# Transformer block on one core: ten steps of the second modulation placed ahead of the first projection group, and the last output tile summed in two column halves

## Chip, cores and metric

One core of one Trainium2 chip. The metric is the device time of one execution in microseconds (us); lower is better. Before the change three timed executions gave 676.25, 676.32 and 678.70 us, median 676.32 us.

## What is computed

One transformer block in fp32 for 512 tokens of width 1024. `D_FF` is 2816. The heads are of three kinds (six with a forget gate, four mLSTM, six block-sparse); only the frame matters here:

```python
mod = jax.nn.silu(c) @ w_ada[l] + b_ada[l]
sh1, sc1, g1, sh2, sc2, g2 = jnp.split(mod[:, None, :], 6, axis=-1)
hn = (_rms(x, norm1_g[l]) * (1 + sc1) + sh1).astype(x.dtype)
y = _mixer(hn, w_in[l], ...)
x = x + g1 * (y.astype(x.dtype) @ w_out[l])
hn = (_rms(x, norm2_g[l]) * (1 + sc2) + sh2).astype(x.dtype)
gate, up = jnp.split(hn @ w_gate_up[l], 2, axis=-1)
x = x + g2 * ((jax.nn.silu(gate) * up) @ w_down[l])
```

The six parts of `mod` are six products of one 1024-vector with 1024x1024 blocks of `w_ada`.

## The kernel before

**Stages.** (1) To about 56 us: the loads of `x`, the first norm, `sh1` and `sc1` on TensorE (PE) from tiles `ada`, and the products for the mLSTM q and k (tile `gT`). Inside this stage each engine's instructions are chained in program order. (2) To about 310 us: 70 numbered steps. Group `A` (mLSTM v and gates) is steps 0 to 7, `F0` to `F2` steps 8 to 31, `B0` to `B2` 32 to 55, `E` 56 to 63, `o0` 64 to 69. A step loads one 128-row weight tile some steps ahead (three are loaded before step 0, `PRE`), splits it into a high part on ScalarE (ACT) and a low part on VectorE (DVE) or GpSimd (POOL), and issues a share of its group's matmuls. Every product is three matmuls (high by high, high by low, low by high: `mm3`). Between the matmuls, `attend` releases the attention and mLSTM work by a table of due times, and `extra` the convolution (`cy`), the gate chain and others. (3) The second norm and the feed-forward, and (4) the down projection, which multiplies by `g2` and adds `x`.

**The second modulation.** The generator `ada` makes `g1` (`ada_row`), then `sc2` and `sh2` (`ada_col`). Each comes in two halves of 512 columns. A half is eight products: a load of 128x512 (256 KB) by SyncE (SP) into one of three buffers (`AST = 3`, tag `ast`), and a DVE instruction that multiplies it by a column of `cs` and, from the second on, adds it to the sum (the first is a TENSOR_SCALAR, the other seven are SCALAR_TENSOR_TENSOR). The ninth step of a half of `g1` loads and adds its bias row; in `sc2` and `sh2` it is empty. The next step starts with one matmul (or four small ones) over the finished sum and its copy out, then the first product of the next half. In all there are 54 steps; in the trace the halves are `g10s`, `g11s`, `sc20s`, `sc21s`, `sh20s`, `sh21s` (loads), and `g`, `sc`, `sh` (sums). From step `ADA0 = 12` on each step of the main loop takes one of them, so the last is taken at step 65.

**Order.** Outside stage 1 the engine queues are filled by the Tile framework's list scheduler, which works on its own estimate of time: of what it holds to be ready on an engine, the instruction that comes first in the program goes first. The place in the program is therefore a rank and not a time, and an instruction can run well ahead of its step. On the chip each queue then runs in the order fixed at build time, waits included. DMAs for stage 2 are all issued by SP.

**The last tile.** `down(j, t)` issues the `mm3` of inner tile `j` (22 of them) for token tile `t` (4) into PSUM bank `gg[t]`. The last `DLAST = 4` inner tiles are done token tile by token tile, so that one tile's output can leave while the next is computed. For the last tile of the second column half, the output (multiply by `g1b`, which by then holds `g2`; add `x1`; store) is in two halves of 256 columns, both after all its matmuls.

Of the kernel before, what the change touches and what calls it, by code (L numbers as in the profile page):

```python
# [18 lines left out]
NT = SEQ // P  # L19
# [3 lines left out]
NJ = DFF // P  # L23
# [16 lines left out]
POSTD = 3.0  # L40
LAG = 3.0
ADA0 = 12
OKT = (0, 1, 2, 5, 3, 4)
PTB = 2
ELEAD = 0.8
# [13 lines left out]
DLAST = 4  # L59
# [71 lines left out]
def hybrid_block_kernel(  # L131
# [6 lines left out]
    V, S, G, TE, SY = nc.vector, nc.scalar, nc.gpsimd, nc.tensor, nc.sync  # L138
    dbg = dbg or {}
    in_order = {k: [1] for k in "VSGTY"}  # L140
    V, S, G, TE, SY = (_InOrder(tc, e, in_order[k]) for e, k in zip((V, S, G, TE, SY), "VSGTY"))
# [62 lines left out]
        for f in rsqrt_ops(y, v, tag):  # L204
            f()

    def mm3(o, ah, al, wh, wl, start, stop):
        TE.matmul(o, ah, wh, start=start, stop=False)
        TE.matmul(o, ah, wl, start=False, stop=False)
        TE.matmul(o, al, wh, start=False, stop=stop)  # L210

    g1b = cp.tile([P, D], F32, name="g1b")
    mod2 = cp.tile([P, 2, 8], F32, name="mod2")
# [342 lines left out]
    def gates_4(Mr):  # L556

        pM = bank("t", "pM")
        for t in range(NT):
            TE.transpose(pM[:, t * 4:(t + 1) * 4], Mr[:, t * P:(t + 1) * P], ident[0:4, 0:4])  # L560
        V.tensor_tensor(em, Fc[:, :, 0:4], pM[:, 0:16].rearrange("p (t g) -> p t g", t=NT), op=ALU.add)
        S.activation(em, em, AF.Exp, scale=-1.0)
        gs["em"] = em
# [39 lines left out]
    def ada_all():  # L603
        yield from ada_row(2 * D, g1b, "g1")
        yield from ada_col(4 * D, "sc2", 0)
        yield from ada_col(3 * D, "sh2", 1)

    ada = ada_all()
# [293 lines left out]
    def add_x1(t, hf_, pb, eng):  # L902
        hs = slice(512 * hf_, 512 * hf_ + 512)
        tm = hp.tile([P, 512], F32, tag="P1", name=f"ot{t}{hf_}", bufs=SB)
        V.tensor_tensor(tm, pb, g1b[:, hs], op=ALU.mult)
        eng.tensor_tensor(x1[t][hf_], x1[t][hf_], tm, op=ALU.add)

    def wo(kc, hf_):
        return w_out[0, kc * P:(kc + 1) * P, 512 * hf_:512 * hf_ + 512]
# [13 lines left out]
    for pr in range(3):  # L923
        add_qkv("B", BQ, pr)
    add_group("E", KTS, lambda kt: w_in[0, kt * P:(kt + 1) * P, MO:MO + 256], 256, hn, after_e)
    add_group("o0", OKT, lambda kt: wo(kt, 0), 512, lambda kt: yT[kt],
              lambda t, pb: add_x1(t, 0, pb, G if O0G else V), BLKO0)
# [16 lines left out]
    for i in range(3):  # L944
        plan_softmax("B", i, 40 + 8 * i, gq8[:, 1:2], prmT[:, 87:88], lambda h: (AL, h), 5 + i)
    queue.sort(key=lambda e: e[:2])
    extra = {GT[0]: [g12], GT[1]: [g3], GT[2]: [g4], GT[3]: [lambda: gates_4(gs["M"])],
             len(steps) - len(OKT) + 2: [load_x1]}
    for m, j in zip((0, 2, 1, 3), CVS):
# [12 lines left out]
    def load_67(hf_):  # L962
        rr = hp.tile([P, 2, 512], F32R, tag="raw", name=f"olr{hf_}", bufs=2)
        load_late(6, hf_, (rr[:, 0], rr[:, 1]))
        load_late(7, hf_, (pairt(f"olh{hf_}"), pairt(f"oll{hf_}")))

    loads = [l for l, _ in steps]
    loads += [lambda: load_67(0)] + [lambda kt=kt: load_late(kt, 1) for kt in OKT] + [lambda: load_67(1)]
    for j in range(PRE):
        loads.pop(0)()  # L970
    for j, (_, half) in enumerate(steps):
        for _ in range(1 if j < len(steps) - LPR else 2):
            loads and loads.pop(0)()
        attend(j)
        half(0)
        attend(j + 0.5)
        for f in extra.get(j, []):
            f()
        half(1)
        if j >= ADA0:  # L980
            next(ada, None)
# [13 lines left out]
    def last_o(t):  # L995
        tsl = slice(t * P, (t + 1) * P)
        for hf_, kts, tag in ((0, (6, 7), "t"), (1, OKT + (6, 7), "g")):
            pb = bank(tag, f"ol{t}{hf_}")
# [103 lines left out]
    def temp(name):  # L1102
        return act_tile(name, F32)
# [216 lines left out]
    for hf_ in range(2):  # L1320
        gg = [bank(tg, f"d{hf_}{t}") for t, tg in enumerate(("gggg", "sstt")[hf_])]

        def down(j, t, hf_=hf_, gg=gg):
            if j % 2 == 0:
                k = NJ // 2 * hf_ + j // 2
                down_load(k + DLD)
                down_split(k + DPR)
            if steps_[0] % 2:
                next(ada2, None)
            steps_[0] += 1  # L1330
            tsl = slice(t * P, (t + 1) * P)
            ah, al, wh, wl = dprep[hf_, j]
            mm3(gg[t], ah[:, tsl], al[:, tsl], wh, wl, j == 0, j == NJ - 1)

        for j in range(NJ - DLAST):
            for t in range(NT):
                down(j, t)
        for t in range(NT):
            for j in range(NJ - DLAST, NJ):
                down(j, t)  # L1340
            parts = 2 if hf_ and t == NT - 1 else 1
            for c_ in range(parts):
                n = 512 // parts
                o = slice(c_ * n, c_ * n + n)
                ho = slice(512 * hf_ + c_ * n, 512 * hf_ + c_ * n + n)
                ot = temp(f"fo{hf_}{t}{c_}")
                V.tensor_tensor(ot[:, :n], gg[t][:, o], g1b[:, ho], op=ALU.mult)
                V.tensor_tensor(ot[:, :n], ot[:, :n], x1[t][hf_][:, o], op=ALU.add)
                SY.dma_start(out[0, t * P:(t + 1) * P, ho], ot[:, :n])
# [39 lines left out]
```

## Time and profile before

| | us |
|---|---|
| median of three runs | 676.32 |
| the profiled execution, own time | 678.59 |
| its span in the trace | 676.8 |
| PE busy | 646.9 (96%) |
| DVE busy | 518.1 (77%) |
| ACT busy | 365.1 (54%) |
| POOL busy | 97.2 (14%) |

The span is what the trace shows of the profiled execution; 1.79 us of its time lie outside of it. A time in a row is counted from the span's start. "Idle before" names what ended the wait ahead of an instruction. PE records overlap, because a matmul starts before the one ahead has drained: the distance from start to start is what one costs in a stream.

### The profile page before, as it was taken

The numbers are of one execution on the slowest core, as the hardware profiler recorded it, in microseconds if no ns is written. First come the engines' busy times: TensorE is split into PE (matmuls) and PEld (weight loads), VectorE is DVE, ScalarE is ACT, GpSimd is POOL, SyncE is SP. The second block draws the span as 40 slices with busy tenths as digits, with TensorE's granted clock in tenths as the row PEclk, the third lists the DMA queues.
The fourth block names the chain that finished last, engine by engine and source line by source line (L and its number), as shares of the span: only waits on it lengthen the run. The fifth ranks groups of instructions, "written<-read, shape, count | busy, mean of one in ns | idle before, by whom it ended". The sixth has DMA issues, their size and how long they took to land.

```text
span 676.8 us, 11779 instructions
## 1 busy us (share of the span) xinstructions
PE 646.9 (96%) x4238; PEld 588.9 (87%) x4238; DVE 518.1 (77%) x1034; ACT 365.1 (54%) x722; POOL 97.2 (14%) x135
## 2 busy tenths in 40 slices
PE   4999899999999999999999999999999999999997
PEld 3678888899999988778999999999999998788885
DVE  3549889969998899888778987888777999448313
ACT  4445478656876777645834554554544665316210
POOL 3012216344252355000000000000000000000000
PEclk9999988999999999999999999999999999999999
DMA  9986736667877667621346433322433237306101
GB/s 270 306 244 166 189 94 145 169 176 205 199 219 180 177 197 189 222 87 33 109 156 219 125 125 125 113 60 78 125 125 126 100 120 225 148 15 214 51 0 62
DMA packets 95549, 99.64 MB, mean 147 GB/s; under 512 B 8186, under 2 KB 70010, under 8 KB 95492
## 3 DMA queue, kind: packets, MB, share of 16 engines
q1 hardware_dynamic: 95492, 98.91, 50.3%
q8 instruction: 33, 0.54, 0.4%
q14 instruction: 24, 0.20, 0.1%
HBM read 84.15 MB, written 2.10 MB: 127 GB/s over the span
## 4 chain that ended last, share of the span: by engine, by line
PE 64%; DVE 19%; ACT 5%; DMA 5%; issue 4%; SPq 2%; POOL 0%; DVEq 0%; ACTq 0%; POOLq 0%
PE d L114 14%; PE B L114 5%; PE F L114 4%; PE ol L114 3%; PE gT L114 2%; DVE g L114 2%; SPq L114 2%; PE f9A L114 1%; PE f8A L114 1%; PE f7A L114 1%; PE f6A L114 1%; PE f5A L114 1%; PE f4A L114 1%; PE f3A L114 1%; PE pc L114 1%
## 5 line engine op out<-in xcount | busy, mean ns | idle before, releaser
L114 ACT ACTIVATE ah<-A 128x512 fp32r<-128x512 f32 x44 | 25.6, 620 | 33.4 <-PE d L114 33.1
L114 DVE TENSOR_TENSOR al<-A,ah 128x512 fp32r<-128x512 f32 x44 | 29.1, 685 | 18.1 <-ACT ah L114 18.1
L114 DVE TENSOR_TENSOR r<-r,r 128x1024 f32<-128x1024 f32 x20 | 24.4, 1220 | 1.5 <-DMA r<-in_w_gate_up_dram 1.2
L114 DVE TENSOR_TENSOR fo<-d,g1b 128x512 f32<-128x512 f32 (+1 forms) x9 | 5.6, 630 | 17.9 <-PE d L114 17.8
L114 ACT ACTIVATE Fp<-Fs,Fmn 128x128 f32<-128x128 f32 (+3 forms) x24 | 12.6, 526 | 9.8 <-DVE Fmn L114 5.6
L114 ACT ACTIVATE u<-u 128x512 f32<-128x512 f32 x20 | 12.5, 627 | 8.1 <-DVE u L114 8.0
L114 ACT ACTIVATE Bp<-Bs,Bmn 128x128 f32<-128x128 f32 (+3 forms) x24 | 12.6, 526 | 7.4 <-DVE Bmn L114 3.5
L114 DVE SCALAR_TENSOR_TENSOR m<-pc,b1sc,prmT 128x1 f32<-128x1 f32 x8 | 1.7, 218 | 19.1 <-PE pc L114 15.7
L114 POOL TENSOR_SCALAR Fp<-Fp,Fls 128x128 f32<-128x128 f32 (+2 forms) x18 | 11.1, 618 | 26.4 <-DVE Fls L114 21.3
L114 PE MATMUL gT<-sq,ident 128*128 128x256 f32 x12 | 5.3, 626 | 9.1 <-ACT sq L114 9.1
L114 DVE TENSOR_TENSOR A<-u,u 128x512 f32<-128x512 f32 x20 | 13.7, 684 | 0.0
L114 POOL TENSOR_SCALAR Bp<-Bp,Bls 128x128 f32<-128x128 f32 (+2 forms) x16 | 8.2, 510 | 34.4 <-DVE Bls L114 25.0
L114 DVE CUSTOM_DVE_ANT_0 Bs<-Bs,mask 128x128 f32<-128x128 f32 (+3 forms) x24 | 11.6, 492 | 1.6 <-PE Bs L114 1.6
L114 DVE TENSOR_TENSOR Bptl<-Bpt,Bpth 128x128 fp32r<-128x128 f32 (+3 forms) x24 | 11.5, 483 | 1.7 <-ACT Bpth L114 1.5
L114 ACT ACTIVATE Fpth<-Fpt 128x128 fp32r<-128x128 f32 (+3 forms) x24 | 10.4, 435 | 4.2 <-PE Fpt L114 4.1
L114 PEld LDWEIGHTS gT<-sq,ident 128*128 128x128 f32 x12 | 3.8, 329 | 10.0 <-issue 9.1
L114 DVE CUSTOM_DVE_ANT_0 Fs<-Fs,mask 128x128 f32<-128x128 f32 (+3 forms) x24 | 11.7, 488 | 1.0 <-PE Fs L114 1.0
L114 POOL TENSOR_TENSOR sml<-E,smh 128x512 fp32r<-128x512 f32 (+1 forms) x8 | 9.0, 1126 | 23.6 <-ACT smh L114 23.6
L114 PE MATMUL Bpt<-ident,Bp 128*128 128x128 f32 x60 | 10.8, 277 | 1.3 <-POOL gmo L114 0.5
L114 ACT ACTIVATE Bpth<-Bpt 128x128 fp32r<-128x128 f32 (+3 forms) x24 | 10.3, 433 | 3.2 <-PE Bpt L114 2.9
L114 DVE TENSOR_TENSOR Fptl<-Fpt,Fpth 128x128 fp32r<-128x128 f32 (+3 forms) x24 | 11.6, 484 | 0.5 <-ACT Fpth L114 0.4
L114 ACT ACTIVATE row<-pc 128x256 f32<-128x256 f32 x8 | 3.1, 382 | 15.7 <-PE pc L114 15.7
(2326 smaller groups left out, 2830.0 us busy)
## 6 DMA issues: line engine op xcount, KB each, us to landing
r<-in_w_gate_up_dram SPq DMA_DIRECT2D x40, 512.0 KB, 3.8
dr<-in_w_down_dram SPq DMA_DIRECT2D x22, 512.0 KB, 5.5
ada<-in_w_ada_dram SPq DMA_DIRECT2D x16, 512.0 KB, 7.2
x<-in_x_dram SPq DMA_DIRECT2D x4, 512.0 KB, 5.6
w0s<-in_w_in_dram SPq DMA_DIRECT2D x8, 256.0 KB, 6.6
g10s<-in_w_ada_dram SPq DMA_DIRECT2D x8, 256.0 KB, 3.6
g11s<-in_w_ada_dram SPq DMA_DIRECT2D x8, 256.0 KB, 2.7
sc20s<-in_w_ada_dram SPq DMA_DIRECT2D x8, 256.0 KB, 4.0
```

The source lines that it names most:

```text
L114: r = f(*a, **k)
```

## The change

Ten calls of `next(ada)` stand between the three early weight loads and the main loop: the eight products of the first half of `g1`, its bias, and then its matmul and copy together with the first product of the second half. The main loop is not changed, so that from step 12 on each step takes what ten steps later took before, and the last is taken at step 55. In the down projection, `down` takes a column range; the last four inner tiles are issued inside the loop over the column parts. For all tiles but the last that is the same order. For the last tile the twelve matmuls of 512 columns become twelve of 256 columns, the output of that half, twelve of 256 columns, the output of the other half. `skip_group_check` is an argument for the builder and no instruction.

```diff
+ADAE = 10
@@
-    def mm3(o, ah, al, wh, wl, start, stop):
-        TE.matmul(o, ah, wh, start=start, stop=False)
+    def mm3(o, ah, al, wh, wl, start, stop, **kw):
+        TE.matmul(o, ah, wh, start=start, stop=False, **kw)
...
     for j in range(PRE):
         loads.pop(0)()
+    for _ in range(ADAE):
+        next(ada)
     for j, (_, half) in enumerate(steps):
@@
-        def down(j, t, hf_=hf_, gg=gg):
+        def down(j, t, o=slice(0, 512), hf_=hf_, gg=gg):
@@
-            mm3(gg[t], ah[:, tsl], al[:, tsl], wh, wl, j == 0, j == NJ - 1)
+            mm3(gg[t][:, o], ah[:, tsl], al[:, tsl], wh[:, o], wl[:, o], j == 0, j == NJ - 1,
+                skip_group_check=hf_ * NT + t == 2 * NT - 1)
@@
         for t in range(NT):
-            for j in range(NJ - DLAST, NJ):
-                down(j, t)
             parts = 2 if hf_ and t == NT - 1 else 1
             for c_ in range(parts):
                 n = 512 // parts
                 o = slice(c_ * n, c_ * n + n)
+                for j in range(NJ - DLAST, NJ):
+                    down(j, t, o)
```

## Rows read from the trace of the kernel before

**Rows 1.** Stretches: stretch, then busy us (instructions) per engine, PE clock, DMA share, GB/s.

```profile
57.00:67.00 10.00, 10.00 (x82) 10.00 (x81) 9.75 (x18) 6.43 (x14) 1.85 (x2) 1.00 0.73 194
67.00:82.00 15.00, 13.97 (x90) 13.35 (x89) 11.29 (x40) 7.03 (x19) 2.95 (x3) 1.00 0.83 215
82.00:92.00 10.00, 8.62 (x41) 8.02 (x40) 8.90 (x15) 5.87 (x17) 3.98 (x3) 0.83 0.46 131
245.00:260.00 15.00, 13.40 (x100) 11.80 (x99) 14.90 (x35) 12.15 (x30) 10.40 (x14) 1.00 0.84 227
270.00:285.00 15.00, 13.69 (x72) 10.53 (x71) 12.52 (x36) 10.13 (x24) 0.85 (x2) 1.00 0.69 233
```

**Rows 2.** Chain that ended last, 240 to 280 us: start, us, work.

```profile
256.99 1.11 DVE sh L114
...
275.68 0.60 DVE ol21l L114
276.47 0.66 PE myt L114 x4
```

**Rows 3.** Modulation products by tile: duration ns min/median/max, first and last start us.

```profile
L114 DVE SCALAR_TENSOR_TENSOR g<-g10s,cs,g x7: 736/742/752, 54.5 to 86.8; 128x512 f32<-128x512 f32 x7
...
L114 DVE SCALAR_TENSOR_TENSOR g<-g11s,cs,g x7: 745/752/1490, 122.2 to 135.3; 128x512 f32<-128x512 f32 x7
L114 DVE TENSOR_SCALAR g<-g11s,cs x1: 483/483/483, 121.4 to 121.4; 128x512 f32<-128x512 f32 x1
...
L114 DVE SCALAR_TENSOR_TENSOR sh<-sh21s,cs,sh x7: 740/832/1162, 243.2 to 259.5; 128x512 f32<-128x512 f32 x7
```

**Rows 4.** Timeline of SP, 46 to 56 us: start, us, issued load, count.

```profile
46.83 1.37 SPq L114 DMA_DIRECT2D g10s<-in_w_ada_dram  x3
51.28 0.80 SPq L114 DMA_DIRECT2D Aw3s<-in_w_in_dram  x2
...
55.57 0.38 SPq L114 DMA_DIRECT2D g10s<-in_w_ada_dram  x1
```

**Rows 5.** Timeline of DVE, 56 to 92 us.

```profile
56.59 0.43 DVE L114 TENSOR_TENSOR Aw3l<-Aw3s,Aw3h 128x270 fp32r<-128x270 f32 x1
...
62.41 0.43 DVE L114 TENSOR_TENSOR Aw7l<-Aw7s,Aw7h 128x270 fp32r<-128x270 f32 x1
...
66.07 0.74 DVE L114 SCALAR_TENSOR_TENSOR g<-g10s,cs,g 128x512 f32<-128x512 f32 x1
...
68.60 0.74 DVE L114 SCALAR_TENSOR_TENSOR g<-g10s,cs,g 128x512 f32<-128x512 f32 x1
69.26 0.48 DVE L114 TENSOR_TENSOR Vm<-A,Vm 128x128 fp32r<-128x128 f32 x2
...
90.84 1.78 DVE L114 TENSOR_TENSOR g<-g,g10b 1x512 f32<-1x512 f32 x1
```

**Rows 6.** Timeline of PE, 60 to 70 us, with the wait before.

```profile
60.91 0.29 PE L114 MATMUL A<-Aw3h,hn3h 128*128 128x270 f32 x1
...
64.83 0.29 PE L114 MATMUL A<-Aw7l,hn7h 128*128 128x270 f32 x1
...
69.70 0.41 PE L114 MATMUL F<-F0w0h,hn0h 128*128 128x384 f32 x1 [1.03 <-DVE Vm L114]
```

**Rows 7.** End of the chain, from 655 us.

```profile
654.80 17.47 PE d L114 x77
```

**Rows 8.** Timeline of DVE at the end.

```profile
672.63 0.41 DVE L114 TENSOR_TENSOR fo<-d,g1b 128x256 f32<-128x256 f32 x1
672.96 0.75 DVE L114 TENSOR_TENSOR fo<-fo,x 128x256 f32<-128x256 f32 x2
```

**Rows 9.** One stretch of the feed-forward, all matmuls of 256 columns (columns as rows 1).

```profile
400.00:500.00 100.00, 100.00 (x836) 100.00 (x835) 83.54 (x87) 50.17 (x60) 0.00 (x0) 1.00 0.34 109
```

**Rows 10.** Timeline of ACT and of weight loads in the second norm's transposes.

```profile
311.40 1.02 ACT L114 ACTIVATE hf<-p,mod 128x256 f32<-128x256 f32 x2 [0.43 <-PE p L114]
312.02 0.20 PEld L114 LDWEIGHTS p<-ident,xn 128*128 128x128 f32 x2 [0.41 <-ACT hf L114]
```

More of the change, by code (lines that the diff above doesn't have):

```diff
@@ L205, in rsqrt_ @@
             f()
-    def mm3(o, ah, al, wh, wl, start, stop):
-        TE.matmul(o, ah, wh, start=start, stop=False)
-        TE.matmul(o, ah, wl, start=False, stop=False)
-        TE.matmul(o, al, wh, start=False, stop=stop)
+    def mm3(o, ah, al, wh, wl, start, stop, **kw):
+        TE.matmul(o, ah, wh, start=start, stop=False, **kw)
+        TE.matmul(o, ah, wl, start=False, stop=False, **kw)
+        TE.matmul(o, al, wh, start=False, stop=stop, **kw)
     g1b = cp.tile([P, D], F32, name="g1b")
```

## The prediction

> **What bounds the kernel now.** I read the page first: PE is busy 96% of the span, so that nothing can be won but PE's idle time and time at the lower clock. Then the stretches, to see where that time is. From 57 to 67 us PE has no gap at all, while DVE is busy 9.75 of 10 us. From 67 to 82 us PE loses 15 - 13.97 = 1.03 us and DVE is idle 15 - 11.29 = 3.71 us. From 82 to 92 us PE loses 1.38 us and runs at a granted clock of 0.83, so some 1.7 us more go there [rows 1]. From 245 to 260 us DVE is full (14.90 of 15 us) and PE loses 1.60 us; from 270 to 285 us PE loses 1.31 us [rows 1]. The chain of waits says whose fault that is: from 240 to 276 us it runs over DVE almost alone, the modulation's sums `sh` among its links, and only then does it go over to PE [rows 2]. So stage 2 has two tight places for DVE that PE pays for: an early one, where group `A` ends and `F0` begins, and a late one around 250 us. The change takes DVE work out of the late one and puts DVE work into the early one.
>
> **The change part by part.** I sum against the profiled execution, 678.59 us (span 676.8 us and 1.79 us around it), and subtract 678.59 - 676.32 = 2.27 us at the end to stand at the median of the runs.
>
> *What moves.* Ten steps hold ten DMAs by SP, ten DVE instructions, one matmul and one copy. But the trace shows that a rank is no time: `g10s`, ranked at steps 12 to 19, is loaded from 46.83 us on, ahead of `Aw3s` that stands before it in the program [rows 4], and its sums run from 54.5 us on [rows 3], when group `A` has hardly begun. So the first three products stay where they are. What gets the better rank is the rest of the half, the five products that now start between 66.07 and 86.8 us [rows 3, 5] and the bias sum at 90.84 us [rows 5]. After them each half takes about the place of the half before it: `g11s` comes out of 121 to 136 us into the gap up to about 105 us, `sc20s` takes its place, and so on, and the place of `sh21s` (243.2 to 259.5 us) is left empty [rows 3].
>
> *Early: 57 to 70 us.* Five products of 0.74 us are 3.70 us, to be put into a stretch where DVE has 0.25 us free [rows 1, 3]. Two of them already lie just ahead of the first `F0` matmul, at 66.07 and 68.60 us [rows 5], so three more are net, 2.2 us. What do they meet? `Aw7l` is ready at 62.41 + 0.43 = 62.84 us and PE takes it at 64.83 us: 1.99 us of slack [rows 5, 6]. The evacuation of group `A` (tile `Vm`) has none: `F0` waits 1.03 us for it [rows 6]. Bounds: 0 (the three go into small gaps, and the ones that stood in front of `Vm` have left it) and +4.0 us (all five products and the bias, 0.3 us undisturbed, in front of what PE needs). I take one product, **+0.7 us**, since two of the three fit into the slack of `Aw7l`.
>
> SP needs a word, because a load that waits for a buffer holds all behind it. The fourth `g10s` load needs the buffer of the first product, which is done when the second starts, at 54.5 us [rows 3]. If it were queued right before `Aw3s` (51.28 us) [rows 4], the weights behind it would come about 3.2 us later. `Aw3l` is done at 57.02 us and taken at 60.91 us [rows 5, 6], 3.89 us of slack, so that costs nothing by itself; without that cover it would cost the 3.2 us. The loads are 256 KB each and the DMA engines are at 0.73 there [rows 1]: no bound.
>
> *Middle: 67 to 121 us.* Gone are three products and the bias: 3 x 0.74 + 1.78 = 4.0 us [rows 3, 5]. New is the second half: 0.48 + 7 x 0.75 + about 0.3 = 6.0 us [rows 3]. The 2.0 us more on DVE stand against 3.71 us of its idle time from 67 to 82 us [rows 1]. I take **0**; bounds -2.0 us (the products run in the gaps, and the stretch of 82 to 92 us gets its DVE time back) and +2.0 us (none of it is absorbed).
>
> *121 to 240 us.* One half for another of the same size: **0**.
>
> *Late: 240 to 285 us.* `sh21s` leaves: 7 x 0.832 + 0.48 = 6.3 us of DVE time [rows 3] out of a chain that is DVE's to 276 us [rows 2]. PE cannot win more than it loses: 1.60 + 1.31 = 2.9 us in the two stretches [rows 1]. I take three quarters, **-2.2 us**, because PE is then nearly without gaps and the attention chain (ACT, POOL) is next; bounds 0 and -2.9 us.
>
> A page of the Trainium skill bears on this. Here `sh` takes 0.83 us in the middle and up to 1.16 us while POOL is busy 10.4 of 15 us, against 0.74 us for `g10s` [rows 1, 3]. The Trainium skill, SBUF — State Buffer, in its summary of who contends for ports, says that a DVE instruction with two SBUF inputs contends with a GpSimd instruction that reads SBUF, and that the later one blocks. The trace agrees: the same instruction is 0.1 to 0.4 us longer beside POOL. By it the move is worth a little more than its undisturbed length; the sum above already has the measured length in it.
>
> *The tail.* A 512-column matmul costs 17.47/77 = 0.227 us from start to start [rows 7], a 256-column one 100/836 = 0.120 us [rows 9]: 24 instead of 12 are 24 x 0.120 - 12 x 0.227 = +0.15 us. Now the last matmul ends at 672.27 us, four DVE instructions follow, and the last one ends at 672.96 + 0.75 = 673.71 us [rows 7, 8]. After the change two follow, one behind the other: 2 x 0.41 us [rows 8] and some 0.04 us between them (an estimate), 0.86 us. If the halves run side by side the end is 672.27 + 0.15 + 0.86 = 673.28 us: -0.43 us. But both halves lie in one PSUM bank. In the second norm, where transposes into one half of a bank follow a read of its other half, the weight load at 312.02 us waits 0.41 us for that read, and starts 0.06 us after it [rows 10]. If the last tile does the same, the first half is summed at 672.27 - 12 x 0.227 + 12 x 0.120 = 670.99 us, its multiplication runs from about 671.01 to 671.42 us, and only 0.06 us later do the other twelve matmuls start: 671.48 + 11 x 0.120 + 0.29 (the record of a matmul of 270 columns [rows 6]) = 673.09 us, and with 0.02 us to start and 0.86 us the end is at 673.97 us: **+0.3 us**. I take that, since the row shows this very pattern; the other end is -0.4 us.
>
> The Trainium skill, PSUM — Partial Sum Buffer, in PSUM bank collisions raise a hardware error, states the rule behind that row: accesses of two engines to one bank and quadrant must be kept apart by a semaphore, whether or not the columns are the same. It speaks against this half of the change, and the row agrees with it. By it the tail is +0.3 us, by free halves -0.4 us.
>
> *Sum.* 0.7 + 0 + 0 - 2.2 + 0.3 = -1.2 us: 677.4 us on the profiled execution, **675.1 us** on the median. Its own range by the bounds, not all at their ends at once, is 673 to 678 us.
>
> **The rivals.**
>
> *A, full relief: 671.7 us.* All 2.9 us of the late stretches come back, the middle gives 2.0 us as the bias sum and three products leave the stretch of the low clock, the early cost is nothing, the tail is +0.3 us: -4.6 us. For it: the chain is DVE's over the whole late stretch. Against it: DVE is full from 57 to 67 us.
>
> *B, group `A` starves: 679.9 us, slower.* One mechanism: the products now rank ahead of the low parts of `Aw3` to `Aw7`, the convolution and the evacuation of `A`, and DVE runs its queue in order. From the third additional product in front of `Aw7l` on (1.99 us of slack are used up) every further one is 0.74 us of PE. At its full price of 4.0 us, with 0.7 us won late (a quarter, since the later schedule is shifted as well) and +0.3 us in the tail: +3.6 us. For it: 9.75 of 10 us busy, and `F0` that waits already. Against it: the loads. A product can't start before its 256 KB are there, and there are three buffers.
>
> *C, nothing moves: 676.6 us.* The scheduler already pulls these products ahead of their steps, so a better rank changes the order little, and PE is busy 96% anyway; only the tail's +0.3 us is left.
>
> **How the numbers follow.** Chances: forecast 0.42, A 0.24, B 0.16, C 0.18. A measurement of this kernel can tell about 0.5% (3.4 us) from no change, so faster means below 672.9 us and slower above 679.7 us. A lies beyond its bound, with the parts that fall short about 0.2 of 0.24; the forecast's low end adds 0.03. B lies on its bound, 0.11, and a reshuffled schedule that hits another place adds 0.02. So faster 0.23, same 0.64, slower 0.13. The range takes in A's price and the most part of what lies between it and B: 671.2 to 679.2 us; about 0.07 is left out below and 0.12 above.
>
> **What would show it.** Early: `g10s` sums all done by 70 us, `F0`'s first matmul at 70 to 71 us instead of 69.70 us. Late: no `sh` sums after about 230 us, DVE below 13.5 of 15 us from 245 to 260 us, and PE's loss in the late stretches below 1 us. Tail: a gap of about 0.5 us in PE between the two halves, the last DVE instruction about 1.7 us behind the end of the first half's matmuls or later. Wrong if the first `F0` matmul comes after 72 us (B), if the sums stand where they stood (C), or if the gate chain around 83 us moves by more than 1.5 us either way, which I hold at zero.

## The result and the profile after

| | before | after |
|---|---|---|
| median, us (6 runs each, same chip) | 676.32 | 686.86 |
| ratio, 95% interval | | 1.0146 [1.0116, 1.0177] |
| the profiled execution, own time, us | 678.59 | 686.46 |
| its span, us | 676.8 | 684.8 |

The change makes the kernel 1.5% slower. The forecast was 675.1 us (671.2 to 679.2).

The page of after by stretches, columns as in [rows 1]:

```profile
67.00:82.00 15.00, 12.61 (x69) 11.98 (x67) 12.41 (x40) 7.37 (x20) 3.77 (x3) 0.89 0.86 212
82.00:92.00 10.00, 7.93 (x44) 6.85 (x44) 8.04 (x14) 3.91 (x9) 2.45 (x2) 0.88 0.46 139
245.00:260.00 15.00, 14.15 (x110) 13.45 (x109) 13.41 (x48) 11.71 (x35) 6.97 (x11) 1.00 0.50 140
270.00:285.00 15.00, 12.81 (x64) 10.28 (x62) 14.53 (x45) 9.69 (x22) 3.49 (x5) 1.00 0.59 178
```

PE loses 2.39 us from 67 to 82 us, where it lost 1.03 us, and the granted clock falls from 1.00 to 0.89 there. From 245 to 260 us it loses 0.85 us where it lost 1.60 us, but the work in that stretch is another, since everything is some 9 us later by then. From 270 to 285 us it loses more than before, and DVE is fuller, though `sh21s` has gone.

A fixed stretch compares different work once the schedule has shifted, so I go by landmarks: the first matmul of a weight tile, and how much later than in before it comes. `mb` is the first matmul that reads the gate chain's result, `Fqt` the first transpose of F's q, `Bqt` that of B's. The last two columns belong to two experiments described below.

| first matmul | before, us | after | `n1_after_narrow` | `n2_after_narrow_loads` |
|---|---|---|---|---|
| F0, tile 0 | 69.70 | +2.75 | +2.57 | +1.76 |
| `mb` | 84.75 | +4.86 | +4.66 | +2.42 |
| F1, tile 4 | 110.84 | +2.86 | +1.23 | -1.02 |
| `Fqt` | 126.31 | +9.31 | +6.28 | +2.62 |
| `Bqt` | 200.24 | +10.09 | +7.05 | +3.10 |
| `o0`, tile 0 | 260.95 | +8.11 | +5.09 | +1.15 |
| `o0`, tile 4 | 283.72 | +9.32 | +6.29 | +2.36 |

By these landmarks the time goes in two places: 4.9 us up to the gate chain, and 6.5 us between F1's tile 4 and `Fqt`. What seems to be made up between the two is PE's order of work: it takes F1's tile 4 earlier among the mLSTM part, whose own first `den` copy (see below) is 6.35 us late by then. From `mb` to `Fqt` 4.4 us are lost in all. From there to 240 us nothing more is lost. About 1.2 us come back where `sh21s` stood, and they are lost again up to tile 4 of `o0`.

One profiled execution is a rough measure. `e1_tail`, described below, has the order of before up to the last tile and stands 0.16 us early at F0 and 1.42 us early at tile 4 of `o0`. And the profiled execution of before is slow in the feed-forward: the offset of after falls from +9.80 to +7.68 us there, that of `e1_tail` from -1.43 to -3.06 us. So the loss is nearer to the 10.5 us of the medians than to the 7.9 us between the two profiled executions.

**The first place.** SP's timeline (start, us, issued load, count), first in before, then in after:

```profile
55.57 0.38 SPq L114 DMA_DIRECT2D g10s<-in_w_ada_dram  x1
57.05 0.81 SPq L114 DMA_DIRECT2D Aw7s<-in_w_in_dram  x2
58.34 0.38 SPq L114 DMA_DIRECT2D F0w0s<-in_w_in_dram  x1
```

```profile
54.91 0.33 SPq L115 DMA_DIRECT2D g10s<-in_w_ada_dram  x1
...
55.80 1.01 SPq L115 DMA_DIRECT2D g10s<-in_w_ada_dram  x2
...
59.02 0.33 SPq L115 DMA_DIRECT2D g10s<-in_w_ada_dram  x1
...
59.87 0.43 SPq L115 DMA_DIRECT2D Aw7s<-in_w_in_dram  x1
60.96 0.33 SPq L115 DMA_DIRECT2D g10s<-in_w_ada_dram  x1
61.33 1.11 SPq L115 DMA_DIRECT2D Aw7s<-in_w_in_dram  x1
...
63.77 0.38 SPq L115 DMA_DIRECT2D F0w0s<-in_w_in_dram  x1
```

SP's waits from 46 to 66 us in after (released by: us in total, times, longest); before has no such line among its waits there:

```profile
SPq L115 <- DVE g L115: 2.1, 4, 0.9
```

The five later loads of `g10s` now stand among the weight loads, and four of SP's waits are for a product that frees one of the three buffers. So the last piece of `Aw7s` is issued at 61.33 us, some 4 us later than in before, and `F0w0s` 5.4 us later. DVE's products, the bias sum and the first product of `g11s` then stand ahead of the evacuation of group `A` (`gt`, `Vm`; timeline of DVE in after):

```profile
64.33 0.75 DVE L115 SCALAR_TENSOR_TENSOR g<-g10s,cs,g 128x512 f32<-128x512 f32 x1
...
65.66 0.67 DVE L115 TENSOR_TENSOR g<-g,g10b 1x512 f32<-1x512 f32 x1
66.27 0.42 DVE L115 TENSOR_TENSOR Aw7l<-Aw7s,Aw7h 128x270 fp32r<-128x270 f32 x1
...
67.88 1.24 DVE L115 TENSOR_SCALAR g<-g11s,cs 128x512 f32<-128x512 f32 x1
...
70.49 0.28 DVE L115 TENSOR_TENSOR Vm<-A,Vm 128x128 fp32r<-128x128 f32 x1
```

And PE in after, with its wait, F0's first matmul and the modulation's matmul:

```profile
66.77 1.02 PE L115 MATMUL g1p<-g,ones 128*128 128x512 f32 x2
...
72.45 0.66 PE L115 MATMUL F<-F0w0h,hn0h 128*128 128x384 f32 x1 [2.39 <-DVE gt L115]
```

This adds up. PE's wait grew from 1.03 us [rows 6] to 2.39 us, `g1p` put 1.02 us into group `A`, and this execution came 0.37 us later to stage 2 anyway: 1.36 + 1.02 + 0.37 = 2.75 us. The other 2.1 us up to `mb` are told under "The clock".

**The second place.** PE at `Fqt`, in before and in after:

```profile
126.31 0.63 PE L114 MATMUL Fqt<-ident,Fraw 128*128 128x128 f32 x4 [1.13 <-DVE den L114]
```

```profile
135.62 0.63 PE L115 MATMUL Fqt<-ident,Fraw 128*128 128x128 f32 x4 [2.90 <-DVE den L115]
```

`Fqt` waits for the copy `den` that ends a stage of the mLSTM part. These copies are the beat of the chain that DVE and ACT run there. The first two of them, in before and in after (timeline of DVE):

```profile
103.31 0.15 DVE L114 COPY den<-mo 128x2 f32<-128x2 f32 x1
...
110.82 0.14 DVE L114 COPY den<-mo 128x2 f32<-128x2 f32 x1
```

```profile
109.66 0.15 DVE L115 COPY den<-mo 128x2 f32<-128x2 f32 x1
...
119.27 0.14 DVE L115 COPY den<-mo 128x2 f32<-128x2 f32 x1
```

7.51 us between them have become 9.61 us. PE waits there too, for DVE's `E` that leads up to the second copy; ahead of the matmuls `ms` in before its longest wait from 100 to 126 us is 0.49 us. PE in after:

```profile
116.41 0.33 PE L115 MATMUL ms<-MIX,K 128*128 128x128 f32 x1 [2.37 <-DVE E L115]
```

**The clock.** Not all of the loss is waiting. Right behind PE's waits of 2.39 us (ahead of F0), 2.07 us (ahead of `mb`) and 2.37 us (ahead of `ms`) the granted clock is at half, the level of 1.2 GHz. Windows of after (columns as in [rows 1]), the first of them from group `A`'s first matmul to `Fqt`:

```profile
56.61:135.62 79.01, 67.62 (x387) 63.44 (x387) 69.41 (x163) 47.68 (x118) 23.38 (x21) 0.91 0.64 173
72.45:75.80 3.35, 3.35 (x11) 3.35 (x12) 3.19 (x12) 3.15 (x10) 1.01 (x1) 0.50 0.84 193
89.60:96.30 6.70, 6.69 (x22) 6.25 (x23) 5.05 (x12) 3.08 (x9) 0.85 (x1) 0.50 0.70 203
116.80:120.20 3.40, 3.40 (x12) 3.39 (x12) 3.40 (x8) 1.70 (x6) 3.40 (x5) 0.50 0.98 282
```

The same of before, and last a window of `e1_tail`:

```profile
56.24:126.31 70.07, 64.42 (x386) 60.14 (x385) 61.37 (x155) 47.46 (x117) 22.23 (x21) 0.95 0.60 154
85.70:89.10 3.40, 3.40 (x12) 3.40 (x12) 2.79 (x7) 1.40 (x6) 0.00 (x0) 0.50 0.68 190
106.20:109.60 3.40, 3.40 (x12) 3.40 (x12) 3.16 (x14) 3.37 (x7) 0.07 (x1) 0.50 0.73 170
```

```profile
85.70:89.10 3.40, 3.40 (x21) 3.16 (x20) 3.15 (x9) 2.36 (x8) 0.00 (x0) 1.00 0.53 140
```

Up to `Fqt` PE is idle for 5.65 us in before and 11.39 us in after, and it runs at half clock for 6.8 and 13.5 us, which costs about half of that. So the 8.9 us that this stretch has grown by are 5.7 us of waiting and some 3.4 us of clock. Of the 2.1 us between F0 and `mb`, 0.7 us are waiting and 1.7 us the clock. The clock is not fixed by the order of work: where before has 12 matmuls in 3.40 us at half clock, `e1_tail` has 21 in the same order at 2.4 GHz. A difference of some 1.7 us between two traces can therefore be a single stretch of lower clock.

### The profile page after: what moved, and what is told of

It reads as the page before. It is cut to its first block, busy times and chain, and to the rows that moved or that the text cites. A ratio compares the mean times of both kernels' runs of the same rounds, so it can differ in the third digit from the quotient of the medians.

```text
span 684.8 us, 11787 instructions
## 1 busy us (share of the span) xinstructions
PE 648.8 (95%) x4250; PEld 593.0 (87%) x4250; DVE 522.5 (76%) x1034; ACT 365.2 (53%) x722; POOL 95.0 (14%) x135
## 4 chain that ended last, share of the span: by engine, by line
PE 70%; DVE 15%; DMA 5%; ACT 5%; issue 4%; SPq 1%; DVEq 0%; ACTq 0%
PE d L115 14%; PE F L115 5%; PE B L115 5%; PE ol L115 4%; PE fp L115 3%; PE gT L115 3%; DVE g L115 2%; PE f9A L115 1%; PE f8A L115 1%; PE f7A L115 1%; PE f6A L115 1%; PE f5A L115 1%; PE f4A L115 1%; PE f3A L115 1%; PE pc L115 1%
## 5 line engine op out<-in xcount | busy, mean ns | idle before, releaser
L115 ACT ACTIVATE smh<-E 128x512 fp32r<-128x512 f32 (+3 forms) x16 | 7.5, 467 | 8.6 <-DVE E L115 8.4
L115 DVE SCALAR_TENSOR_TENSOR cy<-qkz,prmT,cy 128x511 f32<-128x511 f32 (+2 forms) x12 | 11.8, 985 | 0.0
```

What stands on the lines that cost most here:

```text
L115: r = f(*a, **k)
```

## The experiments

### The parts of the change, one at a time

`e1_tail` has only the last tile in two halves, `e2_steps` only the ten steps.

```diff
+    for _ in range(10):      # e2_steps; not in e1_tail
+        next(ada)
```

> Only the last output tile in two column halves; the modulation steps stand as before. Theory 'halves share a bank': TensorE waits about 0.5 us between the halves and the time is 0.3 to 0.6 us above before (676.6 to 676.9 us). Rival 'halves run side by side': no gap, 0.4 us below before (675.9 us). Either way the tail explains less than a tenth of the 10.5 us.

> Only the ten modulation steps ahead of group A; the last tile as before. Theory 'the steps carry the loss': about 686 us, +9.5 to +10.5 us over before. Rival 'the two parts add up in equal shares': about 681 us.

Measured: `e1_tail` 677.23 us beside 677.08 us, ratio 1.0000 [0.9986, 1.0014]; `e2_steps` 684.90 us, 1.0109 [1.0082, 1.0136], its landmarks those of after within 0.5 us up to 290 us. The ten steps carry the loss, the tail nothing that can be measured in the times; in the trace of `e1_tail` the second half's matmuls wait 0.52 us for the first half's multiplication. `e2_steps` stays below the 9.5 us that were expected. Its interval and that of after overlap, so that the 2.6 us between after and the two parts together are not clear of noise.

`e3_first_half` makes the ten steps early but leaves the other halves at their old steps in the program; `e4_later` makes nothing early, but takes two steps of `ada` in each of the main loop's steps 12 to 21, so that the later halves stand where the change puts them.

```diff
-        if j >= ADA0:                                            # e3_first_half
+        if j >= ADA0 + 10:
             next(ada, None)
-        if j >= ADA0:                                            # e4_later
-            next(ada, None)
+        for _ in range((j >= ADA0) + (ADA0 <= j < ADA0 + 10)):
+            next(ada, None)
```

> The ten steps ahead of group A, but all later halves at the steps where they stood before (the main loop takes its first step at 22), so that only the first half of g1 has moved. Theory 'two places': the first F0 matmul is some 2.5 us later as in the changed kernel, the stretch from 105 to 140 us is as before, and the time is 679 to 681 us. Rival 'all of it is the early stall, which drags the rest': 685 to 687 us. Rival 'all of it is the middle, the early stall is absorbed': 676 to 677 us.

> No early burst: from step 12 to 21 two modulation steps per step of the main loop instead of one, so that every half from the second on stands where the changed kernel has it, and the first half nearly where it was. Theory 'two places': the first F0 matmul stays at 69.7 us, the loss comes between 85 and 140 us, and the time is 680 to 683 us. Rival 'all of it is the early stall': 676 to 677 us, or 674 to 675 us with the relief around 250 us.

Measured: 682.86 us (1.0073 [1.0052, 1.0093]) and 684.15 us (1.0095 [1.0063, 1.0127]) beside 677.08 us. Either half of the move alone costs 5.8 and 7.1 us, both together 7.8 us (`e2_steps`): they don't add, both lose it between F1's tile 4 and `Fqt`. In `e4_later` F0 comes 0.31 us early, F1's tile 4 comes 4.05 us early, and `Fqt` is 4.94 us late, so the early delay is not needed for that.

`e3_first_half` did not separate the first half from the others. Its steps are the old ones, but the queue is not: `g11s` stands as early as in after, and only from `sc20s` on do the halves stand where the steps put them (by tile, first and last start last):

```profile
L114 DVE SCALAR_TENSOR_TENSOR g<-g11s,cs,g x7: 743/746/1230, 79.3 to 106.1; 128x512 f32<-128x512 f32 x7
```

```profile
L114 DVE SCALAR_TENSOR_TENSOR sc<-sc20s,cs,sc x7: 732/751/1155, 160.8 to 178.7; 128x512 f32<-128x512 f32 x7
```

It still loses 6.8 us between F1's tile 4 (+3.17 us) and `Fqt` (+9.95 us), with no product of `sc20s` in that stretch. From the first to the second `den` copy it is 9.61 us as in after, DVE waits 3.65 us in all for ACT's `nl` ahead of the later copies, and PE runs at half clock from 118.4 to 128.6 us. So the products and loads of `sc20s` are not needed for a loss in the second place. (3.69 us of the offsets of `e3_first_half` stand ahead of group `A`, where this execution ran at half clock from 19.4 to 26.2 us; F0 is at +6.18 us.) Both kernels lie above the ranges of the theory of two places.

### Smaller moves

`e5_later_pair` takes two steps at a time in 28 to 37, `e6_one_later` and `e6_one_earlier` shift everything by one step (`ADA0` 13 and 11), `e7_three` makes three steps early, which are those that run early in before as well.

```diff
+        for _ in range((j >= ADA0) + (28 <= j < 38)):   # e5_later_pair
-ADA0 = 12
+ADA0 = 13                                             # e6_one_later; 11 in e6_one_earlier
+    for _ in range(3):                                # e7_three
+        next(ada)
```

> The ten steps' lead is made up late: from step 28 to 37 two modulation steps per step of the main loop (in the trace of before that is 135 to 170 us, where DVE has its most idle time); up to step 27 nothing moves. Theory 'place decides': nothing changes up to 135 us, the modulation leaves the stretch around 250 us, and the time is 674 to 677 us. Rival 'any change of the order costs several us because the whole schedule is refilled': 680 us or more.

> Control: every modulation step one step later (first at 13), no work moved by more than one step. Theory 'place decides': 676 to 678 us. Rival 'any change of the order costs': 680 us or more.

> Control: every modulation step one step earlier (first at 11). Theory 'place decides': 676 to 678 us. Rival 'any change of the order costs': 680 us or more.

> Only three steps ahead of group A, those whose sums run at 54 to 56 us before the change too; the later steps are three steps earlier than before. Theory 'the five products after them are what hurts group A': the first F0 matmul within 0.5 us of 69.7 us, and 676 to 679 us. Rival 'the lead itself hurts, by its size': 678 to 680 us, with the loss after 100 us.

Measured, beside 676.38 us: 682.30 us (1.0084 [1.0057, 1.0110]), 684.58 us (1.0113 [1.0084, 1.0141]), 686.89 us (1.0149 [1.0124, 1.0174]) and 685.99 us (1.0132 [1.0104, 1.0160]). A shift by one step in either direction costs 8.2 and 10.5 us, about as much as the whole change. And it costs it elsewhere: `e6_one_later` is at -0.34 us at `Fqt` and loses 2.95 us up to B0's first tile and 3.4 us between the first and the fifth tile of `o0`; `e5_later_pair` loses its 5 us between 155 and 224 us; F0 of `e7_three` is at +0.06 us, as expected, and its time is above both expected ranges. Part of this is the clock: in each of its two stretches `e6_one_later` runs 3.4 us at half clock (146.9 to 150.3 and 280.0 to 283.4 us), some 1.7 us each, and PE waits 1.5 and 2.1 us more than in before. No account that has one tight place in it can hold for all of these. A theory that is left: the scheduler, given another rank for the modulation, puts other instructions elsewhere too. In after 116 of the 984 DVE instructions that are not the modulation's stand elsewhere, and 85 in `e6_one_later`.

### The order of all other work held

Four kernels test that. In `p1_fixed_after`, `p2_fixed_pair` and `p3_fixed_earlier` every instruction that is not the modulation's is chained, on its engine and without a semaphore, to the one that stood ahead of it in before; only the modulation's own instructions are placed by the scheduler, after the edit of after, `e5_later_pair` and `e6_one_earlier`. In `p4_narrow_late` all instructions are chained so, the modulation's too, and the seven later products of `sh21s` work on 8 columns, which leaves out part of that sum: its eight products take 3.68 us of DVE instead of 6.78 us.

```diff
+    _fix(tc, dict(PE=TE._made, DVE=V._made, Activation=S._made, Pool=G._made, SP=SY._made))
@@ p4_narrow_late
-                V.scalar_tensor_tensor(acc, s_, cs[:, k:k + 1], acc, op0=ALU.mult, op1=ALU.add)
+                n = 8 if name == "sh21" else 512
+                V.scalar_tensor_tensor(acc[:, :n], s_[:, :n], cs[:, k:k + 1], acc[:, :n], op0=ALU.mult, op1=ALU.add)
```

> The ten steps ahead of group A as in the changed kernel (last tile as before), but on all five queues everything that is not modulation is held in the order it has in the kernel before; only the modulation's own instructions are placed anew among it. Theory 'the reshuffle of the other instructions carries the loss': 676 to 680 us. Rival 'the modulation's work at its new places carries it': 683 to 687 us, with the first F0 matmul at 72 us or later.

> The lead made up from step 28 to 37 (two steps per step), everything that is not modulation held in its order of before. Theory 'the reshuffle carries the loss': 674 to 677 us, against 682.3 us for the same edit with the order free. Rival 'the places of the work carry it': 680 to 683 us.

> Every modulation step one step earlier, everything else held in its order of before. Theory 'the reshuffle carries the loss': 676 to 678 us, against 686.9 us for the same edit with the order free. Rival 'the places of the work carry it': 683 us or more.

> All queues in the order of the kernel before, modulation included; seven of the eight products of the last half (sh21) are narrowed from 512 to 8 columns (that part of the sum is left out), so that about 5 us of DVE time go away between 243 and 260 us and nothing else changes. It measures the term 'late relief' of the prediction by itself. Theory 'the relief is worth what PE loses there': 2 us faster (674 to 675 us). Rival 'PE does not gain, other chains end last': 676 to 677 us.

Measured, beside 677.36 us: 692.05 us (1.0221 [1.0165, 1.0277]), 684.02 us (1.0106 [1.0072, 1.0140]), 690.46 us (1.0203 [1.0155, 1.0250]). With the others held the loss stays: the move of after is clearly slower than in `e2_steps`, the other two are no faster than with the order free. So the theory that the reshuffle carries the loss falls. Whether the scheduler's moves soften it is not shown, because the modulation's own instructions stand at other places too: products 2 to 4 of `g11s` start at 71.4 to 77.3 us in `p1_fixed_after`, at 75.6 to 91.5 us in after. In `p1_fixed_after` F0's first matmul is at +5.09 us:

```profile
67.35 0.42 DVE L141 TENSOR_TENSOR Aw7l<-Aw7s,Aw7h 128x270 fp32r<-128x270 f32 x1
...
73.43 0.28 DVE L141 TENSOR_TENSOR Vm<-A,Vm 128x128 fp32r<-128x128 f32 x1
```

```profile
74.79 0.66 PE L141 MATMUL F<-F0w0h,hn0h 128*128 128x384 f32 x1 [3.03 <-DVE Vm L141]
```

The first fence is DVE's timeline, the second PE's: `Aw7l` stands 4.9 us later than in [rows 5], and group `A`'s evacuation behind it.

`p4_narrow_late` is at 676.47 us, 0.9983 [0.9962, 1.0005]. In its trace the offset against before goes from +0.67 us at B2's first tile to -0.88 us here:

```profile
260.07 0.40 PE L141 MATMUL o<-o0w0h,y0h 128*128 128x512 f32 x1
```

That is 1.55 us, but `e1_tail`, where nothing was taken out, goes from -0.90 to -1.40 us between the same two landmarks. So the 3.1 us taken out are worth 1.0 to 1.55 us in the trace and about 1 us in the times (the interval holds no change as well). What was taken out is less than half of the late work; the worth of all of it was not measured by itself.

### What DVE's time costs

Is it DVE's time that costs so much? In four kernels every instruction of before is chained in its old place. Three of them have three extra reductions of a constant tile on DVE, of 0.68 us each, early, in the mLSTM part, or behind it. The fourth makes the seven later products of `g11s` narrow (2.43 us of DVE for this half instead of 6.95 us).

```diff
+    for _ in range(3):   # d1_early, d2_mid, d3_idle, at places in DVE's chain
+        V.tensor_reduce(du, mask.rearrange("p (g d) -> p g d", g=4), op=ALU.add, axis=AX.X)
@@ d4_narrow_mid
+                n = 8 if name == "g11" else 512
```

> The kernel before, with all instructions of the five queues held in the order of before, and three extra VectorE instructions put between them: each reduces a constant tile of 512 columns to 4 columns that nobody reads (about 0.7 us, worked out from the 0.40 us of a reduction over 256 columns). They stand between AL and the low part of Aw7, the place that the prediction gave to its three net products. The prediction's early term says +0.7 us, since two of three fit into the slack of Aw7l. The theory that VectorE's queue from there on to the mLSTM part is one chain says +1.5 to +3 us, with F0's first matmul about +1.5 us and the den copies at 103 to 126 us later by as much. The theory that the loads or the reordering are the cause says 0.

> The same three extra VectorE instructions, one each after E11 (about 101 us), after the low part of F1w7 (about 112 us) and after the second den copy of the first head pair (about 119 us), everything else in the order of before. The prediction's middle term (2 us of work go into VectorE's gaps) says 0. The chain theory says +1.5 to +3 us, all of it there at the first transpose of the F group's q (Fqt, 126.31 us in before). The loads or the reordering as cause: 0.

> The same three extra VectorE instructions after the den copy, and among the sums of squares of the third F tile (146 to 150 us), behind the mLSTM chain, where VectorE has gaps; everything else in the order of before. The chain theory says under +0.5 us. If any small shift at all costs this kernel several microseconds further on, as the controls with the order left free make one think, it is +2 us or more here too.

> All instructions in the order of before, but the seven later products of g11 (121 to 136 us) work on 8 columns and not on 512, which leaves out that part of the sum: some 5 us of VectorE work are gone from the mLSTM chain's stretch, the loads stay. The chain theory says -2 to -4 us, with the den copy at 126.01 us and Fqt some 2 us sooner. That VectorE does not matter there: 0.

Measured, beside 676.84 us: 678.02 us (1.0015 [0.9994, 1.0037]), 678.34 us (1.0024 [1.0004, 1.0045]), 678.41 us (1.0032 [1.0016, 1.0048]) and 676.98 us (0.9999 [0.9981, 1.0017]). The extra work by tile in the first two (duration ns min/median/max, first and last start):

```profile
L141 DVE TENSOR_REDUCE du<-mask x3: 675/681/685, 59.6 to 64.0; 128x4 f32<-128x512 f32 x3
```

```profile
L141 DVE TENSOR_REDUCE du<-mask x3: 672/675/677, 100.6 to 120.0; 128x4 f32<-128x512 f32 x3
```

2.0 us of DVE time cost PE 0.85 us between the start of stage 2 and F0 in the first, 1.2 us between F0 and `Fqt` in the second, 1.4 us between F2's fifth tile and B0 in the third, and nothing grows behind that. So the chain theory (1.5 to 3 us in the first two, under 0.5 us in the third) fails in the third. The theory of a kernel that any shift upsets is not excluded by the time of the third (2.2 us, interval 1.1 to 3.2 us, where it said 2 us or more), but by its trace: the loss stands where the work stands and not further on. In the traces about half of what is added to DVE reaches PE, wherever it stands; the times say 1.0, 1.6 and 2.2 us, each with an interval of more than 1 us either way. 4.5 us taken out between 121 and 137 us bring nothing (`Fqt` -0.27 us against F0). In after eleven more products and one more bias than in before stand ahead of the `den` copy that `Fqt` waits for (4 of `g11s`, 7 of `sc20s`): 10 x 0.75 + 0.48 + 0.67 = 8.65 us. At the traces' 0.4 to 0.7 us for a microsecond that is 4 to 6 us, not 9.3.

### The order of after held, its work taken out

The last two kernels chain every instruction in the order of after. `n1_after_narrow` makes the 21 later products of `g10s`, `g11s` and `sc20s` narrow. `n2_after_narrow_loads` shortens their loads as well.

```diff
+                n = 8 if name in ("g10", "g11", "sc20") else 512        # both
+                V.scalar_tensor_tensor(acc[:, :n], s_[:, :n], cs[:, k:k + 1], acc[:, :n], op0=ALU.mult, op1=ALU.add)
+            n = 8 if k and name in ("g10", "g11", "sc20") else 512      # n2_after_narrow_loads
+            SY.dma_start(s_[:, :n], w_ada_v[:, k, c0:c0 + n])
```

> The changed kernel with all its instructions held in its own order on all five queues, but the later seven products of g10, g11 and sc20 (54 to 135 us) work on 8 columns and not on 512, which leaves out that part of three sums: some 13 us of VectorE work are gone ahead of 137 us, the loads keep their size, their buffers and their places on SP's queue. If VectorE's time is the cause, F0's first matmul goes back to about 70 us, Fqt to about 126 to 129 us and the time to about 677 to 680 us. If the loads or the order of all the other instructions are the cause, Fqt stays at 133 us or later and the time at 683 us or more.

> The kernel of the run before (the changed kernel's own order held, the later seven products of g10, g11 and sc20 on 8 columns, which leaves out that part of three sums), and the 21 loads of these products fetch 8 columns too, 4 KB and not 256 KB; each load keeps its place on SP's queue, its buffer and its wait for it. If the length of the loads and the traffic is the cause, VectorE no longer waits for them, F0's first matmul comes at 71 us or sooner, Fqt at 129 us or sooner, and the time is 681 us or less. If it is the order of the queues with its waits, Fqt stays at 131 us or later and the time at 683 us or more.

Measured: 685.43 us beside 676.98 us (1.0140 [1.0118, 1.0161]) and 681.24 us beside 676.38 us (1.0078 [1.0053, 1.0104]). Without the products' time F0 is nearly as late as in after, `Fqt` comes at 132.59 us, and 8.5 of the 10.5 us are still there: it is mostly the loads or the order. The 2.0 us less are not clear of noise, since the intervals of the two ratios overlap. In the trace, `Fqt` is 3.0 us earlier than in after, but PE waits only 0.6 us less up to there; it runs 6.8 us at half clock instead of 13.5 us. DVE then stands and waits for the loads (`n1_after_narrow`, DVE):

```profile
64.64 0.23 DVE L141 SCALAR_TENSOR_TENSOR g<-g10s,cs,g 128x8 f32<-128x8 f32 x1 [1.11 <-DMA g10s<-in_w_ada_dram]
...
129.20 0.23 DVE L141 SCALAR_TENSOR_TENSOR sc<-sc20s,cs,sc 128x8 f32<-128x8 f32 x1 [1.65 <-DMA sc20s<-in_w_ada_dram]
```

With the loads short as well, another 3.6 us go, in the times as at `Fqt`, and PE waits 3.1 us less up to there, at the same time at half clock. The time is 0.2 us above the 681 us that the loads as the cause were to give, F0 comes at 71.46 us, above their 71 us, and `Fqt` at 128.93 us, just inside their 129 us. What is left is mostly order; the matmul `g1p` in group `A` and the narrow products, most of them 0.2 us each, are there too. `n2_after_narrow_loads`, DVE:

```profile
67.60 0.64 DVE L141 TENSOR_SCALAR g<-g11s,cs 128x512 f32<-128x512 f32 x1 [1.36 <-PE g1p L141]
...
105.78 0.15 DVE L141 COPY den<-mo 128x2 f32<-128x2 f32 x1
...
109.22 0.67 DVE L141 TENSOR_TENSOR g<-g,g11b 1x512 f32<-1x512 f32 x1
...
109.90 0.54 DVE L141 TENSOR_TENSOR F1w7l<-F1w7s,F1w7h 128x384 fp32r<-128x384 f32 x1
...
115.38 0.15 DVE L141 COPY den<-mo 128x2 f32<-128x2 f32 x1
```

The sum has one buffer: the first product of `g11s` may not overwrite it before `g1p` has read it, and `gt` and `Vm`, which F0 needs, queue behind that product. And from the first to the second `den` copy it is 9.60 us, just as in after, with the long products out of the way: the bias sum and the low part of `F1w7`, which in before come at 141.30 and 111.34 us, behind the second copy, now stand ahead of it. PE in the same kernel:

```profile
112.52 0.33 PE L141 MATMUL ms<-MIX,K 128*128 128x128 f32 x1 [2.36 <-DVE E L141]
...
128.93 0.63 PE L141 MATMUL Fqt<-ident,Fraw 128*128 128x128 f32 x4 [0.28 <-DVE den L141]
```

The wait of after in the middle is still there (2.37 us), that at `Fqt` is gone (2.90 us). Taken together nothing is lost in this kernel from `mb` (+2.42 us) to `Fqt` (+2.62 us): what the order costs between the first two `den` copies is made up ahead of `Fqt`, with the long products gone. What stays at `Fqt` was there at `mb` already.

## Why the prediction was wrong

The step that failed is **"Middle: 67 to 121 us ... I take 0"**, with the bounds of 2.0 us either way; what lies just behind it, **"121 to 240 us ... 0"**, failed up to `Fqt`. The sum has -1.2 us where the profiled executions differ by +7.9 us and the medians by +10.5 us. In place of the 0, PE waits 5.7 us more between the start of group `A` and `Fqt`, part of it in the early place, and loses some 3.4 us more to the lower clock.

**What bounds the kernel.** That PE pays for DVE's queue in an early and a late place was right. But I named the places by PE's loss, and the second place is one where before lost only 1.13 us, at `Fqt`. The stretches of the groups in [rows 1] leave out 92 to 245 us, and with them the mLSTM chain.

**Early: +0.7 us, bounds 0 to +4.0 us.** It came to +2.75 us at F0, within the bounds. I counted three net products; in after seven instructions of the modulation stand ahead of the first `Vm` where one stood: five products, the bias, and the first of `g11s`. Three extra instructions really cost 0.85 us (`d1_early`), near my 0.7 us. The matmul `g1p` in group `A` (1.02 us) and the single buffer of the sum were not in the sum at all. For that buffer DVE waits 1.36 us in `n2_after_narrow_loads`; in after no wait is recorded, but the first product of `g11s` takes 1.24 us there and 0.48 us in before [rows 3]. The bias's 0.3 us undisturbed, in the upper bound and in the middle, stands in no row; it took 0.67 us in after.

**SP.** The mechanism was named, and its price for one load, 3.2 us, was set against the slack of `Aw3l`. Four loads wait, 2.1 us in all, and what stands behind them is `Aw7`, whose slack I had given as 1.99 us, and F0's weights, 5.4 us late. (The row at 60.91 us is of the high part of `Aw3`; the low part is taken at 61.03 us, which changes nothing.) Loads carry more than products: taken out of the order of after, the loads' length gives back 3.6 us in the times, and 4.9 us stay with the order and what is left of the work. The products' time gives 2.0 us by the medians (10.5 to 8.5 us), which is not clear of noise. By landmarks at `Fqt` it is 3.7, 2.6 and 3.0 us of 9.3 us, the last mostly the clock. These are single steps taken in one order, and I haven't tried them in another.

**Middle: 0.** The idle 3.71 us of DVE from 67 to 82 us [rows 1] lay for the most part in the gate chain's own waits for PE (1.59 us for `pF` and 0.80 us for `pR` in before, 2.96 us for `pF` in after), and work can go there only if the queue has it at that point. What I said would prove me wrong did: the gate chain came 4.9 us later, 2.75 us of it up to F0 and the rest mostly the lower clock behind PE's longer wait. I had priced that clock only where before had it, from 82 to 92 us. What was lost behind the gate chain I had not considered: PE waits 2.37 us ahead of `ms` and 2.90 us at `Fqt`, with a third stretch at half clock between them. In the order of after the wait at `Fqt` is that of the long loads (2.33 us with narrow products, 0.28 us with short loads too); `e3_first_half` shows that another order loses as much without `sc20s`. The wait ahead of `ms` belongs to the order between the `den` copies, 2.1 us longer from the first to the second in after, in both kernels with narrow products and in `e3_first_half`. That the products' time carries a share is not shown.

**121 to 240 us: 0.** From `Fqt` on that is so for this kernel, +9.31 us there and +9.30 us at E's first tile (236.94 us). It was no safe term: `e5_later_pair`, `e6_one_later`, `p2_fixed_pair` and `p3_fixed_earlier` lose 4.6 to 7.7 us between `Fqt` and E.

**Late: -2.2 us.** Right in kind: the last product of `sh` starts at 234.1 us, and the stretch has 13.41 us of DVE, as said. In size it was about 1.2 us in after, and 1.0 to 1.55 us for the 3.1 of 6.8 us that `p4_narrow_late` took out. I took three quarters of PE's loss in two stretches, and it was less than half. That GpSimd makes the products longer holds in part: two of the seven of `sh21s` ran 0.6 to 0.8 us beside it and took 0.74 to 0.75 us. In after the relief did not last: PE in after,

```profile
286.34 0.55 PE L115 MATMUL Bpt<-ident,Bp 128*128 128x128 f32 x3 [1.27 <-DVE Bptl L115]
```

waits for DVE again, which was busy 14.53 of 15 us just before, from 270 to 285 us.

**Tail: +0.3 us.** Right. DVE and PE at the end of after:

```profile
678.74 0.42 DVE L115 TENSOR_TENSOR fo<-d,g1b 128x256 f32<-128x256 f32 x1
...
680.95 0.42 DVE L115 TENSOR_TENSOR fo<-d,g1b 128x256 f32<-128x256 f32 x1 [1.32 <-PE d L115]
681.41 0.42 DVE L115 TENSOR_TENSOR fo<-fo,x 128x256 f32<-128x256 f32 x1
```

```profile
679.22 0.39 PE L115 MATMUL d<-dw118h,ah 128*128 128x256 f32 x1 [0.52 <-DVE fo L115]
```

The other half's matmuls begin 0.06 us after the multiplication of the first half ends, as in [rows 10]. From the start of `d` to the last DVE instruction it is 127.32 us instead of 126.87 us: +0.45 us. The Trainium skill's rule that the prediction cites (PSUM — Partial Sum Buffer, PSUM bank collisions raise a hardware error) says the same of two halves in one bank; the trace agrees, with 0.52 us of waiting.

**The rivals.** B was the nearest, and its sign was right: slower, by VectorE's queue ahead of group `A`'s end. Its decision point was passed, since six more instructions stood there and not three. But its mechanism, `A` starving for `Aw7l`, is not what the trace shows: the matmuls of `A` run without a gap, and what comes late is the evacuation behind them. And its 679.9 us held only the early place. With 0.16 for it, 0.13 for slower and an upper end of 679.2 us I gave too little to a mechanism that I had seen at work in before, where F0 already waited.

**Open.** Why one step of shift costs 8 to 10 us (`e6_one_later`, `e6_one_earlier`) was settled in part. Against before both run 6.8 us longer at half clock, worth about 3 us each; the rest is PE's waiting, and what sets it was not taken apart. The loads' places in SP's queue and the order between the `den` copies are candidates; these runs took them apart for the order of after only. No run held the clock, so how much of its 3.4 us each wait brings is open.

## What to carry to other kernels

Work that is moved as a bundle is priced by everything its queue holds behind it: a load that waits for one of three buffers, the single buffer of a sum, the matmul and the bias at its end. Price each against the slack of what stands directly behind it in that queue, not against the mean idle time of an engine. Look at the granted clock behind every new wait of TensorE before you put the whole difference of two traces down to waiting. To learn whether time, traffic or order costs, hold the order and take out one of the three; adding the same small work at several places shows in the same way what an engine's microsecond is worth there.

## What was unexpected

In this kernel a microsecond added to DVE, which is busy 77% of the span, cost PE 0.4 to 0.7 us at each of three places in the traces (0.85, 1.2 and 1.4 us for 2.0 us), in a stretch with idle time as well as in a full one; yet 4.5 us taken out of DVE between 121 and 137 us gave nothing (0.9999 [0.9981, 1.0017]). And the same addition to the bias row, one partition of 512 columns, took 0.67 us in after and 1.78 us in before [rows 5]. In before it began at 90.84 us while GpSimd's `sml` ran (90.74 to 92.08 us) and ended 0.54 us behind it; in after nothing of GpSimd's ran beside it. No run tried this by itself.
